# A two-layer hybrid backbone on one core: layer 2's adaLN moved to VectorE, the last down projection made token-major, and Fourier features taken two steps later

## The chip, the cores and the metric

The kernel runs on one core of a Trainium2 chip. The metric is the device time of one execution in microseconds (us), median of several executions. Engines are named as the profile names them: PE (TensorE, matmul), PEld (its weight loads), DVE (VectorE), ACT (ScalarE), POOL (GpSimd), SP (SyncE, which issues most DMAs).

## The reference, cut to what matters

Two layers over 256 context and 256 latent tokens of width 1024. Each layer normalizes, shifts and scales the tokens by six adaLN vectors of its own, mixes tokens in three branches (attention, Fourier, recurrence), and applies a ConvFFN:

```python
mx = jnp.split((silu_c @ w_ada[l] + b_ada[l])[:, None, :], N_MOD, axis=-1)   # latent: six vectors of 1024
mc = jnp.split(silu_cc @ w_ada[l] + b_ada[l], N_MOD, axis=-1)                # context
hx = modulate(rms_norm(x, norm_mix[l]), mx[0], mx[1])
x = x + mx[2] * merge(attention, fourier, recurrence, gates, w_out[l])
x = x + mx[5] * conv_ffn(modulate(rms_norm(x, norm_ffn[l]), mx[3], mx[4]), w_up[l], cw, cb, w_down[l])
# conv_ffn: u = depthwise_conv3(h @ w_up); up, gate = split(u); return (gelu(gate) * up) @ w_down
# in layer 1 the context tokens take the same steps with mc; layer 2 updates latent tokens only
return rms_norm(x, final_norm)
```

Layer 2 needs the context's vectors only for its first two chunks (shift and scale of the mixer's norm), and those of the latent tokens for all six. `w_ada[l]` is 1024 x 6144 (24 MB), `w_up` 1024 x 5632, `w_down` 2816 x 1024.

## The kernel before, in words

**Layout.** The residual stream `xr` is channel-major: eight tiles of 128 channels x 512 tokens. Every float32 product is made of three matmuls over high and low parts (`gemm`, L137): a weight tile is loaded by SP into one of three "raw" buffers (`chunk`, L161; `load`, L173, which also calls a tick), and `unit` (L192) splits it into a high part (cast, ACT) and a low part (subtraction, DVE), in a pool of three buffers each. So a tile of 128 output channels over 1024 inputs is 24 matmuls; with 512 tokens each has 512 columns, with 256 tokens (layer 2's second half) 256.

**Order of the work.** The order on each engine is fixed when the program is built, from priorities in program order; the DMAs of SP stay in program order. Layer 1's mixer runs to about 461 us of the profile, its output projection to 511; the first ConvFFN runs from 511 to 889 us (eight up/gate pairs of tiles, the first half of the down products with `down(0, 14)`, three more pairs, then `down(14, NF)`, L1142); layer 2's latent projections follow to 925, its attention to 1004, Fourier, merging and recurrence to 1172, output projection to 1199, and the second ConvFFN to the end (1404.5), in the same two halves.

**adaLN.** `ada_steps` (L354) makes one third of a layer's vectors: for each of eight row tiles of 128 rows it loads 128 x 2048 of `w_ada` (1 MB) and makes four float32 products with the two conditioning vectors `cvec` as a 32-column stationary block, side by side in one bank; a copy by DVE, four transposes and two bias adds end it. It is a generator: each `next` does one row tile. `spread(steps, rate)` (L398) makes every weight load advance the steps by `rate`. For layer 2, the first third runs in the first ConvFFN at rate 0.4 behind three empty steps, the parameters of layer 2 and `final_gains`, and what is left is emitted at its last down tile (L1167). The other two thirds (`steps_mix`, L1298) run in layer 2's mixer: one step per finished head in attention (`weighted`, L842) and at rate 0.5 in the merges.

**Attention and Fourier features.** `attention` (L771) walks over eight items (head pairs and heads) in steps k: scores of item k, transposes of item k - 1, weighted values of item k - 2. `FILLS[1]` says at which steps the Fourier features (`features`, L672, 2 x 3 steps: a load, then two groups of 24 matmuls) are put in.

**Down projection and end.** `finish` (L1095) makes the last down products of tile m (stationary: 128 x 128 of `w_down`; moving: 256 or 512 tokens of `gT`), then `residual` on DVE and the squares. In layer 2 `to_tokens` (L1212) scales each tile by the final gain and transposes it to token-major, and at the end the sum of squares is made on PE, and the rows are scaled and stored. `ffn` (L1119) uses five PSUM banks "mm" for projections and down products.

## Time and profile before

| | |
|---|---|
| median of 3 runs | 1407.57 us (1404.57 to 1408.45) |
| profiled execution | 1406.22 us, of which the span from the first to the last instruction is 1404.5 us |
| mean granted TensorE clock | 0.992 |
| PE / DVE / ACT / POOL busy | 1369.5 / 851.3 / 687.8 / 196.2 us |
| HBM | 193.5 MB read, 139 GB/s over the span |

All stretches below are in microseconds from the span's start. Matmuls are pipelined: the duration of a row is from the first column in to the last out, and the distance of two starts is what a matmul costs in a dense stream. "PEclk" is the granted clock as a share of 2.4 GHz.

### The profile page before, as it was taken

How to read it: one execution, taken by the hardware profiler on the slowest of the kernel's cores; microseconds unless marked ns; L12 is line 12 of the kernel's file. 1: busy time of each engine (PE TensorE's matmuls, PEld its weight loads, DVE VectorE, ACT ScalarE, POOL GpSimd, SP SyncE). 2: the span in 40 equal slices, each digit the busy share in tenths (PEclk: the TensorE clock that was granted, in tenths of full speed). 3: DMA queues.
4: the chain of work that ended last, by engine and by line, in shares of the span. 5: the costliest groups of instructions: out<-in, count | busy, mean ns of one | idle time of the engine just before them, and what ended most of it. 6: DMA issues, size and time to landing. Idle time of an engine off the chain costs nothing.

```text
span 1404.5 us, 20928 instructions
## 1 busy us (share of the span) xinstructions
PE 1369.5 (98%) x8362; PEld 1168.4 (83%) x8362; DVE 851.3 (61%) x1417; ACT 687.8 (49%) x1163; POOL 196.2 (14%) x195
## 2 busy tenths in 40 slices
PE   7999999999999999999999999999999999999997
PEld 6676598888888898888888877877788889999997
DVE  4587656656634565555543453778576676777575
ACT  5475635424523444444322442566477855566354
POOL 2011002003200111211100111010111222122012
PEclk9999999999999999999999999999999999999999
DMA  9423733223233502223243337225666766455643
GB/s 332 144 99 133 273 114 98 79 91 105 76 105 105 180 31 90 66 93 112 79 135 95 112 108 259 65 74 197 184 207 191 224 186 205 136 193 168 196 142 99
DMA packets 187937, 195.94 MB, mean 140 GB/s; under 512 B 9372, under 2 KB 178322, under 8 KB 182720
## 3 DMA queue, kind: packets, MB, share of 16 engines
q1 hardware_dynamic: 186624, 193.23, 43.3%
q0 software_dynamic: 1216, 1.38, 0.3%
q8 instruction: 65, 1.06, 0.3%
q14 instruction: 32, 0.26, 0.1%
HBM read 193.54 MB, written 1.05 MB: 139 GB/s over the span
## 4 chain that ended last, share of the span: by engine, by line
PE 90%; DVE 4%; DMA 3%; ACT 2%; issue 1%; SPq 0%; ACTq 0%; DVEq 0%
PE proj L129 54%; PE down L129 8%; PE out L129 7%; PE lat L129 4%; PE pa L129 4%; PE uf L129 2%; PE sc L129 2%; PE pv L129 2%; PE gt L129 1%; PE pt L834 1%; DMA raw<-in_w_ada_dram 1%; DMA raw<-in_w_down_dram 1%; PE kn L129 1%; PE v L129 1%; DMA raw<-in_w_in_dram 1%
## 5 line engine op out<-in xcount | busy, mean ns | idle before, releaser
L158 DVE TENSOR_TENSOR wl<-raw,wh 128x1024 fp32r<-128x1024 f32 (+9 forms) x339 | 335.5, 1003 | 190.5 <-ACT wh L151 186.3
L129 PE MATMUL proj<-hh,wh 128*128 128x512 f32 (+1 forms) x1232 | 416.3, 338 | 1.1 <-ACT hh L478 1.1
L129 PE MATMUL proj<-hh,wl 128*128 128x512 f32 (+1 forms) x1232 | 415.6, 338 | 1.8 <-DVE wl L158 1.8
L129 PE MATMUL proj<-hl,wh 128*128 128x512 f32 (+1 forms) x1232 | 415.9, 338 | 0.0
L151 ACT CAST wh<-raw 128x1024 fp32r<-128x1024 f32 (+7 forms) x307 | 249.6, 833 | 291.3 <-PE proj L129 168.8
L129 PEld LDWEIGHTS proj<-hh,wl 128*128 128x128 f32 x1232 | 234.8, 191 | 27.1 <-DVE wl L158 2.7
L129 PEld LDWEIGHTS proj<-hh,wh 128*128 128x128 f32 x1232 | 235.0, 191 | 26.5 <-ACT hh L478 1.3
L129 PEld LDWEIGHTS proj<-hl,wh 128*128 128x128 f32 x1232 | 234.9, 191 | 24.6
L1199 POOL TENSOR_TENSOR gate<-gate,up 128x512 f32<-128x512 f32 (+1 forms) x44 | 55.3, 1256 | 444.4 <-ACT gate L1198 423.7
L129 PE MATMUL down<-gTh,wh 128*128 128x512 f32 (+1 forms) x224 | 75.5, 337 | 0.0
L129 PE MATMUL down<-gTh,wl 128*128 128x512 f32 (+1 forms) x224 | 75.4, 337 | 0.0
L129 PE MATMUL down<-gTl,wh 128*128 128x512 f32 (+1 forms) x224 | 75.3, 336 | 0.0
L158 DVE TENSOR_TENSOR gTl<-gate,gTh 128x512 fp32r<-128x512 f32 (+1 forms) x44 | 24.6, 559 | 78.5 <-ACT gTh L151 78.5
L129 PE MATMUL pa<-raw,cvec 128*32 128x512 f32 (+1 forms) x576 | 63.9, 457 | 2.4 <-DMA raw<-in_w_ada_dram 2.4
L444 POOL TENSOR_TENSOR sq<-sq,sq 128x256 f32<-128x256 f32 (+1 forms) x28 | 31.6, 1128 | 201.1 <-ACT sq L442 201.1
L151 ACT CAST gTh<-gate 128x512 fp32r<-128x512 f32 (+1 forms) x44 | 22.6, 514 | 51.3 <-POOL gate L1199 51.3
L129 PE MATMUL out<-mh,wl 128*128 128x256 f32 (+1 forms) x152 | 47.4, 312 | 0.0
L129 PE MATMUL out<-mh,wh 128*128 128x256 f32 (+1 forms) x152 | 47.4, 313 | 0.0
L129 PE MATMUL out<-ml,wh 128*128 128x256 f32 (+1 forms) x152 | 47.4, 312 | 0.0
L129 PEld LDWEIGHTS down<-gTh,wh 128*128 128x128 f32 x224 | 42.5, 190 | 4.5
L129 PEld LDWEIGHTS down<-gTh,wl 128*128 128x128 f32 x224 | 42.5, 190 | 4.4
L129 PEld LDWEIGHTS down<-gTl,wh 128*128 128x128 f32 x224 | 42.5, 190 | 4.3
(288 smaller groups left out, 2631.6 us busy)
## 6 DMA issues: line engine op xcount, KB each, us to landing
raw<-in_w_up_dram SPq DMA_DIRECT2D x44, 1024.0 KB, 5.1
raw<-in_w_ada_dram SPq DMA_DIRECT2D x40, 1024.0 KB, 5.0
raw<-in_w_in_dram SPq DMA_DIRECT2D x30, 1024.0 KB, 5.6
raw<-in_w_down_dram SPq DMA_DIRECT2D x16, 896.0 KB, 5.1
raw<-in_w_ada_dram SPq DMA_DIRECT2D x32, 256.0 KB, 7.2
raw<-in_w_in_dram SPq DMA_DIRECT2D x16, 512.0 KB, 5.0
raw<-in_w_out_dram SPq DMA_DIRECT2D x8, 1024.0 KB, 5.2
raw<-in_w_down_dram SPq DMA_DIRECT2D x16, 512.0 KB, 3.9
```

The lines of the kernel that those rows point to most:

```text
L129: pinned(nc.tensor.matmul(o, lhsT, rhs, start=start, stop=stop))
L151: nc.scalar.copy(out, in_)
L158: (lo_eng or nc.vector).tensor_tensor(lo, src, hi, op=ALU.subtract)
L444: eng.tensor_tensor(self.terms[0][:, r], self.terms[0][:, r], sq[:, r], op=ALU.add)
L834: nc.tensor.transpose(o[:, c], probs[i][:, kt * P : (kt + 1) * P], ident)
L1199: nc.gpsimd.tensor_tensor(g, g, us[z], op=ALU.mult)
```

## The change

Five things. (1) Layer 2's adaLN is no longer made of matmuls with a 32-column block. `ada_vector` takes jobs of 512 columns by 1024 rows (both conditionings) or 1024 by 1024 (latent only); a chunk is 512 rows x 512 columns (1 MB). For each 128 rows, DVE multiplies the 128 x 512 weights by the conditioning value of that row (a scalar per partition) and adds them to an accumulator in SBUF; eight such operations make a sum per partition, and `summed` adds the partitions up with eight products of a 128 x 128 block with a column of ones, one job later, and adds the bias. There are four jobs of the first kind and four of the second: 24 chunks, 128 operations on DVE, 64 products on PE. (2) All of it runs in the first ConvFFN, at 2 steps per weight load in place of 0.4, behind the parameters and ten empty steps; layer 2's mixer has no such steps left. (3) In layer 2 the Fourier features' second half is put in at step 8 of attention, before at step 6. (4) Layer 2's down products are token-major: stationary is `gT` (128 tokens), moving are 512 columns of `w_down`, whose rows are loaded two row tiles at a time (1 MB); they accumulate in four banks over the whole loop, two tiles per pair from the second pair's turn on, the last four tiles after the loop; projections keep three banks. (5) The residual is transposed to token-major in the loop (`token_major`), gate and final gain are spread to rows, and the end is made in token-major: multiply, add, square with a sum per row, root, scale, store.

```diff
-FILLS = ({12: 1}, {2: 3, 6: 3})
+FILLS = ({12: 1}, {2: 3, 8: 3})
...
+            if tag != "rows" and i < 3:
+                yield
+                yield
...
+    def ada_vector(l, jobs):
+        cols = columns_of[l]
+        def fetch(job, i):
+            c0, half = job[0][i]
+            src = a["w_ada"][l][half * 512 : (half + 1) * 512, c0 : c0 + 512]
+            return chunk(src.rearrange("(k p) c -> p k c", p=P), 4, 512)
+        def summed(quarters, two):
+            o = bank("pa", "e")[:, 0:16].rearrange("p (g u r) -> p g u r", g=4, u=2)
+            for g, (z, c, *_) in enumerate(quarters):
+                for u in range(2):
+                    mm(o[:, g, u, :], two[z][:, c + u * P : c + (u + 1) * P], ones, True, True)
+            for g, (z, c, s, j) in enumerate(quarters):
+                blk, f = j // 16, j % 16
+                nc.vector.tensor_tensor(
+                    adas[l][blk][:, s, f : f + 2], o[:, g, :, 0], cols["b_ada"][:, j : j + 2], op=ALU.add
+                )
+        sums = None
+        for n, job in enumerate(jobs):
+            halves, quarters, todo = job
+            v = fetch(job, 0)
+            yield
+            accs = [slot("acc", t, F32) for t in ("aa", "ab")]
+            for i, (c0, half) in enumerate(halves):
+                after = fetch(job, i + 1) if i + 1 < len(halves) else None
+                for k in range(4):
+                    for z, s in todo[i]:
+                        w, sc = v[:, k, :], cvec[:, 4 * half + k, s : s + 1]
+                        if half == 0 and k == 0:
+                            nc.vector.tensor_scalar(accs[z], w, sc, None, op0=ALU.mult)
+                        else:
+                            nc.vector.scalar_tensor_tensor(accs[z], w, sc, accs[z], op0=ALU.mult, op1=ALU.add)
+                    if k == 1 and len(todo[i]) > 1:
+                        yield
+                if i == 0 and sums:
+                    summed(*sums)
+                v = after
+                yield
+            sums = quarters, accs
+        yield
+        summed(*sums)
...
+    def ada_both(chunk_of, part):
+        c0 = chunk_of * D + part * 512
+        quarters = [(s, o, s, (c0 + o) // P) for s in range(2) for o in (0, 256)]
+        return ((c0, 0), (c0, 1)), quarters, [[(0, 0), (1, 1)]] * 2
+    def ada_latent(chunk_of):
+        c0 = chunk_of * D
+        quarters = [(z, o, 1, (c0 + z * 512 + o) // P) for z in range(2) for o in (0, 256)]
+        return (
+            tuple((c0 + z * 512, half) for z in range(2) for half in range(2)),
+            quarters,
+            [[(z, 1)] for z in range(2) for _ in range(2)],
...
-            spread(steps, 0.4)
+            spread(steps, 2.0)
...
+        def row_of(cols):
+            t = slot("row", "row", F32, D)
+            for z in range(2):
+                o = bank("rowb", "mm")
+                for i in range(4):
+                    j = 4 * z + i
+                    mm(o[:, i * P : (i + 1) * P], cols[:, j : j + 1].to_broadcast([P, P]), ident, True, True)
+                nc.scalar.copy(t[:, z * 512 : (z + 1) * 512], o)
+            return t
...
+        def token_major():
+            rows_["gain"] = slot("row", "row", F32, D)
+            nc.gpsimd.dma_start(rows_["gain"], a["final_norm"].unsqueeze(0).to_broadcast([P, D]))
+            rows_["gate"] = row_of(ada_cols[2][:, 1, 8:16])
+            yield
+            rows_["x"] = [slot("xt", "row", F32, D) for _ in range(2)]
+            for tt in range(2):
+                for z in range(2):
+                    o = bank("xtb", "mm")
+                    for i in range(4):
+                        nc.tensor.transpose(
+                            o[:, i * P : (i + 1) * P], xr[4 * z + i][:, CTX + tt * P : CTX + (tt + 1) * P], ident
+                        )
+                    nc.scalar.copy(rows_["x"][tt][:, z * 512 : (z + 1) * 512], o)
+                yield
...
+        def down_weights(k, tag=None):
+            v = chunk(a["w_down"][l][k * P : (k + 2) * P, :].rearrange("(k p) c -> p k c", p=P), 2, D)
+            return [[x[:, 0] for x in unit(v[:, z : z + 1], tag)] for z in range(2)]
+        def down_part(k, w, tt, z):
+            if not accs:
+                accs.extend([bank("acc") for _ in range(2)] for _ in range(2))
+            q, c = slice(tt * P, (tt + 1) * P), slice(z * 512, (z + 1) * 512)
+            gemm(accs[tt][z], [(gT[k][0][:, q], gT[k][1][:, q], w[0][:, c], w[1][:, c])], k == 0, k == NF - 1)
+        def down_tokens(k):
+            ws = down_weights(k)
+            for i in range(2):
+                for tt in range(2):
+                    for z in range(2):
+                        down_part(k + i, ws[i], tt, z)
...
+        def down_last(k):
+            ws = {}
+            for k2 in range(k, NF, 2):
+                ws[k2], ws[k2 + 1] = down_weights(k2, "wd")
+            t = small.tile([P, 1], F32, tag="warm", name=nm("warm"), bufs=1)
+            nc.scalar.activation(t, gT[-1][1][:, 0:1].bitcast(F32), AF.Sqrt, bias=eps, scale=0.0)
+            first = NF - 2
+            for k2 in range(k, first):
+                for tt in range(2):
+                    for z in range(2):
+                        down_part(k2, ws[k2], tt, z)
+            ys, yg = [[[slot("y", "y", F32) for _ in range(2)] for _ in range(2)] for _ in range(2)]
+            ssq = small.tile([P, 2, 2], F32, tag="ssq", name="ssq", bufs=1)
+            for tt in range(2):
+                for z in range(2):
+                    for k2 in range(first, NF):
+                        down_part(k2, ws[k2], tt, z)
+                    with prio(150):
+                        c, y = slice(z * 512, (z + 1) * 512), ys[tt][z]
+                        nc.vector.tensor_tensor(y, accs[tt][z], rows_["gate"][:, c], op=ALU.mult)
+                        nc.vector.tensor_tensor(y, y, rows_["x"][tt][:, c], op=ALU.add)
+                        junk = slot("sq", "s", F32)
+                        nc.scalar.activation(junk, y, AF.Square, accum_out=ssq[:, tt, z : z + 1])
+                        e = nc.vector if tt and z else nc.gpsimd
+                        e.tensor_tensor(yg[tt][z], y, rows_["gain"][:, c], op=ALU.mult)
+                with prio(150):
+                    r = small.tile([P, 1], F32, tag="ry", name=nm("ry"), bufs=2)
+                    nc.vector.tensor_tensor(r, ssq[:, tt, 0:1], ssq[:, tt, 1:2], op=ALU.add)
+                    nc.scalar.activation(r, r, AF.Sqrt, bias=eps, scale=1.0 / D)
+                    nc.vector.reciprocal(r, r)
+                    nc.vector.tensor_scalar(yg[tt][0], yg[tt][0], r, None, op0=ALU.mult)
+                    nc.scalar.activation(yg[tt][1], yg[tt][1], AF.Copy, scale=r)
+                    for z in range(2):
+                        nc.sync.dma_start(out[0, tt * P : (tt + 1) * P, z * 512 : (z + 1) * 512], yg[tt][z])
...
+        if last:
+            side = token_major()
+            with phase("ffn", gT=16, c=8, row=4, wd=8, y=8):
+                with banks(acc=4, mm=3):
+                    next(side)
+                    for i in range(0, NF, 2):
+                        pair_of_tiles(i)
+                        if 2 <= i < NF - 2:
+                            down_tokens(i - 2)
+                        if i >= 4:
+                            next(side, None)
+                    down_last(NF - 4)
+            return
...
-    steps = chain(iter([None] * 3), params(1, nc.gpsimd), final_gains(), ada(1, 0))
+    for b in range(1, 3):
+        nc.gpsimd.memset(adas[1][b], 0.0)
+    par1 = params(1, nc.gpsimd)
+    parts_of = lambda chunks: [ada_both(c, part) for c in chunks for part in range(2)]
+    vec1 = ada_vector(1, parts_of((0, 1)) + [ada_latent(c) for c in range(2, 6)])
+    steps = chain(iter([None] * 2), islice(par1, 2), iter([None] * 8), par1, vec1)
...
-    steps_mix = chain(ada(1, 1), ada(1, 2))
```

## Rows read from the trace of the kernel before

**Rows 1.** The page, busy time of the engines (us, share, instructions), and its chain by engine
```profile
PE 1369.5 (98%) x8362; PEld 1168.4 (83%) x8362; DVE 851.3 (61%) x1417; ACT 687.8 (49%) x1163; POOL 196.2 (14%) x195
...
PE 90%; DVE 4%; DMA 3%; ACT 2%; issue 1%; SPq 0%; ACTq 0%; DVEq 0%
```

**Rows 2.** Stretch, length, busy us (count) of PE, PEld, DVE, ACT, POOL; PEclk, DMA share, GB/s
```profile
511.30:686.20 174.90, 174.90 (x816) 146.49 (x816) 98.74 (x125) 75.92 (x101) 26.08 (x28) 1.00 0.28 88
686.20:763.10 76.90, 76.90 (x341) 63.30 (x340) 30.79 (x66) 19.38 (x23) 1.36 (x2) 1.00 0.37 110
...
925.00:1004.20 79.20, 77.63 (x498) 58.49 (x498) 58.51 (x135) 45.33 (x114) 7.09 (x9) 0.98 0.39 130
1004.20:1107.00 102.80, 102.65 (x722) 91.97 (x722) 72.26 (x93) 77.21 (x105) 16.57 (x16) 1.00 0.68 209
1107.00:1131.00 24.00, 22.22 (x165) 18.79 (x164) 15.32 (x21) 18.54 (x26) 8.22 (x9) 1.00 0.57 178
...
1369.40:1404.50 35.10, 27.06 (x217) 25.71 (x215) 19.37 (x39) 15.65 (x32) 8.01 (x8) 0.94 0.32 98
```

**Rows 3.** The same by stretch, of the instructions on adaLN's tile pa alone, summed
```profile
sum 619.70, PE 30.53 PEld 4.51 DVE 1.38 ACT 0.00; mean PE 3.82 PEld 0.56 DVE 0.17 ACT 0.00
...
925.00:1004.20 79.20, 13.72 (x64) 1.91 (x64) 0.69 (x1) 0.00 (x0) 0.98 0.39 130
```

**Rows 4.** Timeline of PE around one row tile: start, duration, instruction
```profile
806.63 0.39 PE L129 MATMUL proj<-hh,wl 128*128 128x512 f32 x1
806.95 1.06 PE L129 MATMUL pa<-raw,cvec 128*32 128x512 f32 x8
...
808.28 0.39 PE L129 MATMUL proj<-hl,wh 128*128 128x512 f32 x1
```

**Rows 5.** Groups by shape: transposes on PE (count, then busy us and mean ns)
```profile
L834 PE MATMUL pt<-ident,pr 128*128 128x128 f32 x160 | 26.5, 278 | 0.0
```

**Rows 6.** PE's waits, 760 to 890 us: in all, times, longest
```profile
PE pa L129 <- DMA raw<-in_w_ada_dram: 1.8, 1, 1.8
```

**Rows 7.** Timeline of PE around four products of a 128x128 block with ones
```profile
912.74 0.28 PE L129 MATMUL lat<-hh,wl 128*128 128x256 f32 x1
913.16 1.02 PE L129 MATMUL ss<-ones,sq 128*128 128x2 f32 x8
...
914.25 0.28 PE L129 MATMUL lat<-hl,wh 128*128 128x256 f32 x1
```

**Rows 8.** Groups on DVE by shape, and one tile's durations (min/median/max)
```profile
L822 DVE TENSOR_SCALAR pr<-pr,rs 128x512 f32<-128x512 f32 x24 | 11.7, 487 | 0.3
...
L479 DVE SCALAR_TENSOR_TENSOR hl<-hf,ada,hh 128x256 fp32r<-128x256 f32 x56 | 26.2, 492 | 0.2 <-ACT hh L478 0.2
...
L512 DVE SCALAR_TENSOR_TENSOR nf<-lr,cols,rb 128x512 f32<-128x512 f32 x7 | 4.9, 745 | 3.2 <-PE rb L129 3.2
...
L953 DVE SCALAR_TENSOR_TENSOR ri<-ri,u x16: 684/692/1125, 222.4 to 1116.9; 128x512 f32<-128x512 f32 x16
```

**Rows 9.** Pieces of the chain: dense streams of 512 and of 256 columns
```profile
708.39 54.71 PE down L129 x241
...
1294.57 40.32 PE down L129 x336
```

**Rows 10.** Timeline of DVE and of POOL, 226 to 229 us
```profile
227.52 1.15 DVE L952 SCALAR_TENSOR_TENSOR ri<-a,ri 128x512 f32<-128x512 f32 x1 [2.92 <-ACT ri L949]
...
226.08 2.04 POOL L951 TENSOR_TENSOR a<-av 128x512 f32<-128x512 f32 x2 [12.11 <-ACT av L947]
```

**Rows 11.** DMA issues: count, size of each, us to landing
```profile
raw<-in_w_ada_dram SPq DMA_DIRECT2D x40, 1024.0 KB, 5.0
```

**Rows 12.** The end: the last down matmul, and the stores
```profile
1396.07 0.28 PE L129 MATMUL out<-gTh,wl 128*128 128x256 f32 x1
...
out_dram<-y SPq DMA_DIRECT2D x4, 256.0 KB, 2.5
```

More of the change, by code (lines that the diff above doesn't have):

```diff
@@ L1 @@
 import math
+from itertools import islice
 from contextlib import ExitStack, contextmanager
@@ L96, in phase @@
             was = {t: where.get(t) for t in tags}
-            where.update({t: (pool, n) for t, n in tags.items()})
+            where.update({t: (pool, n, t) for t, n in tags.items()})
             yield
@@ L297, in spread_out @@
             pp = bank("pp", "lat" if tag == "rows" and i == 0 else "e")
[L298 removed]
+            ins = nc.tensor.transpose(pp[:, 0:n], rows4[0:n, i, :], ident[0:n, 0:n])
+            if tag == "rows":
+                tc.keep_in_program_order(ins)
             cols = par.tile([P, n], F32, tag=f"cols{i}", name=nm("cols"))
@@ L1027, in project_out @@
             first()
-            finish(held, merged, ranges(t0), gate, t0, squares, None, then)
+            finish(held, merged, ranges(t0), gate, t0, squares, then)
         def out_units():
@@ L1093, in ranges, with finish @@
         return [slice(r.start - t0, r.stop - t0) for r in streams(t0)]
-    def finish(held, xs, qs, gate, t0, squares, also=None, then=None, cut=0):
+    def finish(held, xs, qs, gate, t0, squares, then=None, cut=0):
         os = [bank("out")[:, 0 : T - t0] for _ in held]
@@ L1143, in down @@
             held, gate = [], ada_cols[2][:, :, 8:16]
-            together = 3 if last else 2
+            together = 2
             for m in range(8):
@@ L1160, in down @@
                     if together - 1 <= m < HELD[l]:
-                        finish(
-                            held, gT[k0:k1], [Y], gate, t0, squares, to_tokens if last else None,
-                            cut=k1 - k0 - 2 if len(held) > 1 else 0,
-                        )
+                        finish(held, gT[k0:k1], [Y], gate, t0, squares, cut=k1 - k0 - 2 if len(held) > 1 else 0)
                     if m == 7:
@@ L1168, in down @@
                             first()
-                        finish(held, gT[k0:k1], ranges(t0), gate, t0, squares, to_tokens if last else None, then)
+                        finish(held, gT[k0:k1], ranges(t0), gate, t0, squares, then)
                 else:
@@ L1180, in first_pair @@
         def first_pair():
-            two = [(next(ups), bank("proj", "mm")[:, 0:W]) for _ in range(2)]
+            two = [(next(ups), bank("proj", "acc" if last else "mm")[:, 0:W]) for _ in range(2)]
             for q in streams(t0):
@@ L1188, in first_pair, with pair_of_tiles @@
             return [conv(o, z, "up") for z, (u, o) in enumerate(two)]
-        with phase("ffn", gT=32, c=8), banks(dict(out="mm"), mm=5, rb=2):
-            for i in range(0, NF, 2):
-                if i == 0:
-                    us = first_pair()
-                else:
-                    us = [conv(project(next(ups), h, X), i + z, "up") for z in range(2)]
-                for z in range(2):
-                    g = conv(project(next(gts), h, X), NF + i + z, "gate")
-                    nc.scalar.activation(g, g, AF.Gelu_apprx_tanh)
-                    nc.gpsimd.tensor_tensor(g, g, us[z], op=ALU.mult)
-                    hi, lo = pair("gT", "gT", W)
-                    split(hi, lo, g)
-                    gT.append((hi, lo))
+        def pair_of_tiles(i):
+            if i == 0:
+                us = first_pair()
+            else:
+                us = [conv(project(next(ups), h, X), i + z, "up") for z in range(2)]
+            for z in range(2):
+                g = conv(project(next(gts), h, X), NF + i + z, "gate")
+                nc.scalar.activation(g, g, AF.Gelu_apprx_tanh)
+                nc.gpsimd.tensor_tensor(g, g, us[z], op=ALU.mult)
+                hi, lo = pair("gT", "gT", W)
+                split(hi, lo, g)
+                gT.append((hi, lo))
+        if last:
[11 more added lines that the diff above has]
+            return
+        with phase("ffn", gT=32, c=8, aa=2, ab=2), banks(dict(out="mm"), mm=5, rb=2):
+            for i in range(0, NF, 2):
+                pair_of_tiles(i)
                 if i == 14:
@@ L1206, in ffn @@
         ticks.clear()
-    fn = const.tile([P, 8], F32, tag="fn", name="fn")
-    ys = []
-    def to_tokens(j):
-        if not ys:
-            ys.extend([slot("y", "h", F32) for _ in range(2)] for _ in range(2))
-        f = slot("yf", "n", F32)
-        nc.vector.tensor_scalar(f[:, 0:SEQ], xr[j][:, CTX:], fn[:, j : j + 1], None, op0=ALU.mult)
-        pt = bank("yt", "rb")
-        for i in range(2):
-            nc.tensor.transpose(pt[:, i * P : (i + 1) * P], f[:, i * P : (i + 1) * P], ident)
-        for i in range(2):
-            c = slice((j % 4) * P, (j % 4 + 1) * P)
-            copy((nc.vector, nc.scalar)[i], ys[i][j // 4][:, c], pt[:, i * P : (i + 1) * P])
     columns_of = [{} for _ in range(DEPTH)]
@@ L1306, in backbone @@
     emit(mix)
[L1307 to L1316 removed]
+    ffn(1, columns_of[1], adas[1], True, h_ffn1, ups1, None, None, None, None)
 _INS = [
```

28 lines of the change are left out of this document (5 added, 23 removed).

## The prediction

> **What bounds the kernel now.** Read the page first: PE is busy 98% of the span, DVE 61%, and the chain that ended last is PE for 90% of its length [rows 1]. So time is PE's instruction stream, and the sum below is made of what enters and leaves that stream, and of holes in it. Next read the table by stage [rows 2]. In the first ConvFFN (511 to 763 us) PE is busy all the time; in layer 2's attention (925 to 1004) and where the branches end (1107 to 1131) there are holes of about 2 us; the last stretch of the kernel (1369 to 1404.5) has 8 us without a matmul, nearly all of it the tail. DVE, which is to get the new work, is busy 98.7 of 174.9 us in the first stretch of the first ConvFFN and 58.5 of 79.2 us in layer 2's attention. The granted clock is 1.00, the upper level of 2.4 GHz, in the first ConvFFN, and 0.98 or more up to 1131.
>
> **Layer 2's adaLN leaves PE.** It was 24 row tiles of four products each; the trace has them as 8 matmuls a tile. PE's busy time with them is 30.5 us over five stretches (187 of the 192 matmuls) [rows 3]; with the last five, 31.5. A look at one tile agrees: the matmul before it starts at 806.63, the next but one after it at 808.28, 1.65 us where 0.45 would do, so 1.2 us a tile [rows 4]. Term: **-31.5**. Twelve transposes of the row sums and one of the final gain go too; a transpose of that shape is 26.5 us by 160 or 0.17 us [rows 5]: **-2**. Between 760 and 890 us PE waits once, 1.8 us, for the chunk of a row tile [rows 6]; the change has fetched all before, so **-2**.
>
> **What comes instead on PE.** Eight jobs each end in eight products of a 128x128 float32 block with a column of ones. The nearest row is the sum of squares: four such products are 8 matmuls in 1.02 us, and set in a stream of 0.12 us matmuls they move it by 1.27 us (912.74 to 914.25, where 0.24 would do) [rows 7]. For 64 products that is 16.3 us at the bare rate and 20.3 at the whole price of each group of four; a job has two groups back to back, so I take 17.5: **+17.5**.
>
> **What comes on DVE.** 128 operations on 128x512 (per job 2 of the two-operand form, 14 with an accumulator). The first form took 487 ns. For the second no row has both its size and a pointer scalar: from SBUF without a pointer it is 692 ns (median), with a pointer at 128x256 it is 492 ns, at 128x512 with one operand in PSUM 745 ns [rows 8]. I take 0.745: 112 x 0.745 + 16 x 0.487 = 91 us, with the small bias adds some 96. Whether PE sees it depends on where it falls. The rate of 2 steps per weight load spends 19 steps on parameters and pauses; the 42 steps of the sum then cover the last 2.75 up/gate pairs before the first down half, that half, and the 3 pairs after it. A pair of tiles is 4 x 24 matmuls at 0.227 us [rows 9], or 21.8 us of PE, plus 1.7 for the new products of 0.8 jobs: 23.5. DVE's own work in a pair is 98.7 / 8 = 12.3 [rows 2]; four steps add 12.8 operations and some adds, 9.6. Sum 21.9, against 23.5. In the down half a load has 9.6 us of PE (76.9 / 8) and 3.9 of DVE, plus 4.9: no conflict.
>
> The 1.6 us left in a pair are not safe. GpSimd multiplies gate and up in a pair twice, today in a gap of DVE. Where GpSimd and DVE ran together, a DVE operation of the form that otherwise takes some 690 ns took 1.15 us, and GpSimd's two took 2.04 [rows 10]. Two such meetings cost a pair some 1 to 2 us and close the gap. The Trainium skill ("GPSIMD Engine Reference", Specifications) says the same: GpSimd shares its SBUF interfaces with VectorE, and they contend when an instruction of DVE has two SBUF inputs; the trace agrees. And DVE executes in order, so an accumulate that waits for its chunk holds the convolutions and the low halves of the weights behind it, and through those PE. The chunks share the three "raw" buffers and SP's queue with the weights, 1 MB each, 5.0 us to landing [rows 11]. Bound from below 0 (DVE fits), from above 20 us, some 3.5 us for each of 5.75 pairs. I take 1 us a pair: **+6**.
>
> **What the removed products had covered.** In layer 2's attention the row tiles stood in places where PE would otherwise have waited for a softmax: 13.7 us of busy time there for 64 matmuls, 1.7 us a tile against 1.2 in a dense stream [rows 3, 4]. Without them PE has some 64 us of work there and DVE 58.5, in step with each other through the score and transpose banks. Items 6 and 7, which have neither projections nor, now, Fourier features, are the likeliest holes; the features, moved to step 8, fill the drain behind the last scores. I give back 4 us of the 13.7 (bounds 0 and 10). From 1004 to 1133 the tiles stood among projections; only at 1107 to 1131, with 1.8 us idle [rows 2], is a recurrence late anyway: 2 back (bounds 0 and 4). Term: **+6**. What runs on SP's queue there loses 16 transfers of 1 MB; nothing waits longer for that.
>
> **The last ConvFFN.** Its down products turn from 528 matmuls of 256 columns at 0.120 us (40.3 / 336), 63.4 us, into 264 of 512 columns at 0.227, 59.9 [rows 9]: -3.5. The 16 transposes of the result and the last sums of squares leave (about -3); 16 transposes of the residual, in the loop, and 8 broadcasts of the gate come (+3, of which the broadcasts may lie in the wait for the norm at 1198). Small waits for weights of the last stretch shrink, since half of the down weights are now loaded among the pairs: -1. The tail stays: today 8.2 us from the last down matmul at 1396.1 to the end, over residual, square, sum, root, scaling and a 2.5 us store [rows 12]; afterwards multiply, add, square, root, scaling and the same store, 7.5 to 8.5. The projections have three PSUM banks in place of five: a bank is held for the 2.9 us of its 24 matmuls and until the convolution on ACT and DVE has read it, behind their other work; no row shows that with three banks, so 0 to 4, taken as +0.5 since five banks left no hole in the loop before. Together **-4**.
>
> **The sum.** -31.5 - 2 - 2 + 17.5 + 6 + 6 - 4 = -10. Against the profiled execution (1406.2 us, 0.1% under the median) that is 1396.2; against the median of 1407.57, **1397.5**.
>
> **Rivals.** *One: DVE becomes the bound of the first ConvFFN.* An accumulate that stands at the head of DVE's queue before its chunk has landed holds DVE for up to the 5 us of a landing. About 14 chunks fall into the 5.75 pairs, which leave DVE 1.6 us each, or 9 us. It decides from 0.7 us a chunk on; at 2.5 us a chunk PE loses 35 - 9 = 26 us instead of 6, and the kernel takes 1417, slower. For it: three raw buffers for two consumers, and a DVE load of 93% before contention. Against: weights are split up to three units ahead, and the chunks are fetched one ahead.
> The Trainium skill has a rule that would end there as well ("Vector Engine (DVE) Microarchitecture Reference", Points that are easy to get wrong): the accumulate form with two SBUF sources that are not bf16 runs at half throughput. The mechanism in rows: 256 more columns cost 745 - 492 = 253 ns; at half throughput 512 columns would cost 506 more, 1.25 us each, a pair 27.5 us of DVE against 23.5 of PE, and the time 1415, or 1423 with the down loads, which then exceed PE too. But the 692 ns of [rows 8] are of this form with two float32 sources in SBUF, so the rows speak against it: 3 in 100, inside this rival's chance.
> *Two: the removed products were only filling.* If attention and branches return 10 + 9 of their 24.5 us rather than 6, the time is 1410, no different. For it: the spread places of the tiles in attention; against: the branches' PE is full (102.65 of 102.80 us) [rows 2].
> *Three: all cover holds.* No stall in the first ConvFFN, 2 given back in place of 6: 1387.5. For it: the averages, and two to three units of lookahead.
>
> **How the numbers follow.** Forecast 0.52, one 0.16, two 0.13, three 0.19. The forecast's own spread is 1392 to 1404. The range reaches to three below and to two above, and stops short of most of one: **1386 to 1411**. A measurement here tells about 0.3% (4 us) from no change. Faster by more than that: nearly all of the forecast and of three, **0.69**; within: two's lower half and the forecast's upper end, **0.14**; slower: one and the rest of two, **0.17**.
>
> **What would show it.** Right: no matmul of a 32-column block on w_ada after 800 us, 128 of two columns in the first ConvFFN for 16 to 20 us; layer 2's attention some 9 us shorter and its branches some 9; the first ConvFFN 8 to 12 us longer in all, DVE over 85% busy in its later pairs; the second ConvFFN about 4 us shorter, with 512-column down matmuls 0.227 us apart. Wrong: PE waiting for the low halves of weights or for convolutions in the first ConvFFN by tens of us, a granted clock under 1.00 there, accumulates near 1.2 us, or attention as long as before.

## The result, and the profile after

The changed kernel takes 1387.0 us (median of 4 runs, 1384.1 to 1387.7) against 1408.0 for the kernel before: a ratio of 0.985 (95% interval 0.982 to 0.987), 21 us faster. The forecast was 10 us (1397.5, in a range from 1386 to 1411). The direction was right and the time lies just inside the range, but the gain that was forecast is half of the one that came.

The page of the changed kernel, its busy times and its chain, answers to [rows 1]:

```profile
PE 1345.7 (97%) x8029; PEld 1161.8 (84%) x8029; DVE 935.8 (68%) x1545; ACT 687.5 (50%) x1160; POOL 200.2 (14%) x194
...
PE 90%; DVE 4%; ACT 2%; DMA 2%; issue 1%; SPq 0%; POOL 0%; ACTq 0%; DVEq 0%
```

PE lost 24 us of busy time, DVE gained 84, and the chain is PE's as before. Where the time went is seen by stage. The first fence is the kernel before, the second the changed one, in the same stages: first ConvFFN, latents with attention of layer 2, its branches, output projection, second ConvFFN to the end (columns as in [rows 2]).

```profile
509.90:889.40 379.50, 376.04 (x1807) 309.29 (x1807) 190.88 (x286) 144.06 (x197) 45.18 (x45) 1.00 0.36 113
...
889.40:1003.40 114.00, 110.67 (x725) 88.20 (x724) 81.33 (x182) 64.19 (x159) 9.72 (x13) 0.98 0.34 112
1003.40:1171.60 168.20, 165.95 (x1221) 150.65 (x1222) 115.81 (x158) 115.65 (x162) 29.89 (x28) 1.00 0.68 209
1171.60:1199.30 27.70, 25.28 (x205) 24.57 (x204) 16.61 (x25) 13.90 (x23) 8.43 (x6) 0.99 0.59 191
1199.30:1404.50 205.20, 197.12 (x1608) 195.63 (x1608) 142.59 (x225) 114.33 (x183) 32.43 (x28) 0.97 0.50 154
```

```profile
511.60:894.40 382.80, 380.79 (x1866) 322.15 (x1866) 282.39 (x447) 144.75 (x198) 44.85 (x40) 1.00 0.50 159
...
894.40:999.00 104.60, 97.60 (x656) 85.83 (x655) 79.07 (x176) 62.16 (x157) 9.78 (x13) 0.97 0.19 53
999.00:1156.20 157.20, 155.32 (x1153) 148.47 (x1154) 114.22 (x152) 115.19 (x162) 33.43 (x28) 1.00 0.55 164
1156.20:1184.80 28.60, 27.67 (x221) 27.02 (x221) 17.55 (x27) 14.78 (x24) 8.96 (x7) 0.97 0.63 203
1184.80:1384.60 199.80, 190.10 (x1338) 178.79 (x1337) 138.05 (x201) 114.65 (x178) 29.79 (x25) 0.98 0.48 159
```

| stage | before | after | difference | the forecast's terms there |
|---|---|---|---|---|
| to the first ConvFFN (same work) | 509.9 | 511.6 | +1.7 | 0 |
| first ConvFFN | 379.5 | 382.8 | +3.3 | +12.5 |
| latents, attention of layer 2 | 114.0 | 104.6 | -9.4 | -10.4 |
| branches of layer 2 | 168.2 | 157.2 | -11.0 | -8.2 |
| output projection, second ConvFFN | 232.9 | 228.4 | -4.5 | -4 |
| sum | 1404.5 | 1384.6 | -19.9 | -10 |

(The forecast's column puts each term where its work lies: row tiles -8.3 / -13.7 / -9.5 by [rows 3], transposes about -0.7 a stage, the wait -2, products +17.5 and VectorE +6 in the first ConvFFN, the holes +4 and +2.) The first row is layer 1, which no edit touches; over the profiles of this study it lay between 509.9 and 513.1, so 1 to 3 us of any profile's difference are that. The first ConvFFN of the same code is 384.4 us in two other profiles (e3, e9). Nine of the ten missing microseconds are in the first ConvFFN.

**There the price of the products and the stalls were both too high.** This is PE around one job's eight products (start, duration, instruction), which answers to [rows 7]:

```profile
666.47 0.39 PE L130 MATMUL proj<-hh,wl 128*128 128x512 f32 x1
666.70 1.84 PE L130 MATMUL pa<-ones,acc 128*128 128x2 f32 x16
668.40 0.49 PE L130 MATMUL proj<-hh,wh 128*128 128x512 f32 x1
668.72 0.40 PE L130 MATMUL proj<-hl,wh 128*128 128x512 f32 x1
```

From 666.47 to 668.72 pass 2.25 us where two matmuls would take 0.45: 1.8 us a job, the same for all eight jobs of the trace, or 14.4, not 17.5. The sum of the stage is then already there: -8.3 - 0.7 - 2 + 14.4 = +3.4, against +3.3 measured. Nothing is left for stalls, within the 1.6 us by which this stage differs between profiles. PE has no wait of its own between 590 and 845 us in this trace.

**VectorE is nearly as full as forecast, and PE does not notice.** Four of the stretches of 22 to 24 us that have sums:

```profile
612.00:634.00 22.00, 22.00 (x99) 18.18 (x98) 19.15 (x25) 8.94 (x12) 3.27 (x2) 1.00 0.62 200
634.00:656.00 22.00, 22.00 (x98) 18.23 (x98) 21.17 (x52) 10.91 (x15) 2.92 (x2) 1.00 0.53 182
656.00:678.00 22.00, 22.00 (x106) 18.49 (x106) 19.10 (x30) 9.83 (x14) 2.67 (x2) 1.00 0.44 144
...
797.00:821.00 24.00, 24.00 (x118) 20.21 (x117) 22.72 (x33) 9.38 (x13) 2.55 (x2) 1.00 0.62 210
```

DVE is busy 87 to 96% of them (third busy number; the forecast had 93% of a pair before contention), PE all the time, with the clock at its upper level. The accumulates, by their tile (least, median and longest duration in ns, first and last start):

```profile
L440 DVE SCALAR_TENSOR_TENSOR acc<-raw,cvec,acc x112: 731/746/1783, 606.4 to 825.1; 128x512 f32<-128x512 f32 x112
```

What DVE waited for between 590 and 845 us, of its waits (total, times, longest):

```profile
DVE acc L438 <- DMA raw<-in_w_ada_dram: 2.8, 5, 0.8
...
DVE acc L440 <- DMA raw<-in_w_ada_dram: 1.0, 2, 0.6
```

The median of 746 ns is the 745 taken from [rows 8]. The chunks held DVE for 3.8 us in all, not 2.5 us each as the first rival had it.

### The profile page after: what moved, and what is told of

The parts are those of the page before. It is cut to its first block, busy times and chain, and to the rows that moved or that the text cites. A ratio compares the mean times of both kernels' runs of the same rounds, so it can differ in the third digit from the quotient of the medians.

```text
span 1384.6 us, 20366 instructions
## 1 busy us (share of the span) xinstructions
PE 1345.7 (97%) x8029; PEld 1161.8 (84%) x8029; DVE 935.8 (68%) x1545; ACT 687.5 (50%) x1160; POOL 200.2 (14%) x194
## 4 chain that ended last, share of the span: by engine, by line
PE 90%; DVE 4%; ACT 2%; DMA 2%; issue 1%; SPq 0%; POOL 0%; ACTq 0%; DVEq 0%
PE proj L130 54%; PE out L130 7%; PE down L130 6%; PE acc L130 4%; PE lat L130 4%; PE pa L130 3%; PE uf L130 2%; PE pv L130 2%; PE sc L130 2%; PE gt L130 1%; PE pt L904 1%; DMA raw<-in_w_ada_dram 1%; PE kn L130 1%; PE v L130 1%; DVE hf L547 1%
## 5 line engine op out<-in xcount | busy, mean ns | idle before, releaser
L440 DVE SCALAR_TENSOR_TENSOR acc<-raw,cvec,acc 128x512 f32<-128x512 f32 x112 | 88.6, 809 | 2.5 <-DMA raw<-in_w_ada_dram 1.0
L514 POOL TENSOR_TENSOR sq<-sq,sq 128x256 f32<-128x256 f32 (+1 forms) x22 | 25.8, 1170 | 178.9 <-ACT sq L512 178.9
L1347 ACT ACTIVATE gate<-gate 128x512 f32<-128x512 f32 (+1 forms) x44 | 23.1, 525 | 54.9 <-DVE gate L1205 54.3
L154 DVE CAST wh<-raw 128x1024 fp32r<-128x1024 f32 x32 | 22.4, 700 | 33.1 <-PE proj L130 32.5
L130 PE MATMUL down<-gTh,wh 128*128 128x512 f32 x112 | 44.1, 394 | 0.0
L130 PE MATMUL down<-gTh,wl 128*128 128x512 f32 x112 | 43.7, 390 | 0.0
L130 PE MATMUL down<-gTl,wh 128*128 128x512 f32 x112 | 43.6, 390 | 0.0
L130 PE MATMUL lat<-hh,wh 128*128 128x512 f32 (+3 forms) x108 | 38.4, 355 | 0.1
```

Source lines behind the costliest of these rows:

```text
L130: pinned(nc.tensor.matmul(o, lhsT, rhs, start=start, stop=stop))
L154: eng.tensor_copy(out, in_)
L440: nc.vector.scalar_tensor_tensor(accs[z], w, sc, accs[z], op0=ALU.mult, op1=ALU.add)
L514: eng.tensor_tensor(self.terms[0][:, r], self.terms[0][:, r], sq[:, r], op=ALU.add)
L1347: nc.scalar.activation(g, g, AF.Gelu_apprx_tanh)
```

## The experiments

Theory S, in e1's words: VectorE's sums are hidden whole, the products cost their bare rate, and the removed row tiles yield all their time. Its figures say less than that: 35.5 us less 14.1 for 128 matmuls at 0.11 would be 21 us, and its 14 to 17 us leave 4 to 7 for holes that it does not name. Theory F is the forecast's account: stalls of 1 us a pair, 17.5 us for the products. Times are medians; "changed" is 1387.0 us, and each run's ratio is against the kernel before, run beside it. The changed kernel was not run beside them; the median of the kernel before moved from 1407.5 to 1408.8 between such groups of runs.

**e1_ada_only.** The kernel before with the first two parts of the change alone (`ada_vector` in the first ConvFFN at rate 2.0):

```diff
-    steps = chain(iter([None] * 3), params(1, nc.gpsimd), final_gains(), ada(1, 0))
-    steps_mix = chain(ada(1, 1), ada(1, 2))
+    steps = chain(iter([None] * 2), islice(par1, 2), iter([None] * 8), par1, final_gains(), vec1)
+    steps_mix = iter(())
```

> The kernel before with layer 2's adaLN on VectorE in the first ConvFFN alone; the last down projection stays channel-major, the Fourier features stay at step 6. Theory S (VectorE's sums are hidden whole, the products on PE cost their bare rate of 0.11 us a matmul, the removed row tiles yield all their time): 14 to 17 us faster than before, 1391 to 1394, first ConvFFN 2 to 5 us longer than before. Theory F (as forecast: 6 us of stalls from VectorE, 17.5 for the products, 6 given back): 6 us faster, 1402, first ConvFFN about 13 us longer.

Measured 1393.6 us against 1407.7: ratio 0.991 (0.989 to 0.993), 14 us faster. Its first ConvFFN is 4.7 us longer than before:

```profile
510.00:894.20 384.20, 382.31 (x1868) 323.01 (x1867) 280.68 (x448) 145.04 (x198) 46.05 (x42) 1.00 0.50 158
```

Both figures are S's, at the lower end of its gain, and neither is F's: the stalls are absent. Attention gave back more than S's words allow (latents and attention 105.7 us, 8.3 less than before).

**e2_down_only** and **e11_down_same_steps.** The kernel before with the token-major down projection alone. The first also lost the two steps of the old final gain, so that the row tiles of adaLN came two steps earlier; the second keeps them in place:

```diff
-    steps = chain(iter([None] * 3), params(1, nc.gpsimd), final_gains(), ada(1, 0))
+    steps = chain(iter([None] * 3), params(1, nc.gpsimd), ada(1, 0))                      # e2
+    steps = chain(iter([None] * 3), params(1, nc.gpsimd), iter([None] * 2), ada(1, 0))    # e11
```

> The kernel before with the token-major last down projection alone; adaLN stays on PE as before, the Fourier features at step 6. Theory S (the last ConvFFN's part adds to the others unchanged): 5 to 6 us faster than before, 1402 to 1403, all of it in the second ConvFFN. Forecast: 4 us faster. Rival: the two parts need each other (PE with the clock at its upper level from an earlier start, fewer transfers before): under 2 us faster.

> The kernel before with the token-major last down projection alone, as in e2_down_only, but with two empty steps where the steps of the final gain stood, so that the row tiles of layer 2's adaLN stand at the same loads of the first ConvFFN as before. If the down projection is worth its 5 us alone and e2_down_only lost them to row tiles that moved (2.9 us in the first ConvFFN), this is 4 to 5 us faster than before: 1402.5 to 1403.5. If the part is worth nothing without the other one: within 2 us of before.

e2 took 1406.1 us, no different from before (0.9994, 0.998 to 1.001); e11 took 1402.0 against 1408.8 (0.995, 0.994 to 0.997), 6.8 us faster. The trace of e2, second and first ConvFFN:

```profile
1205.20:1404.90 199.70, 189.65 (x1339) 178.08 (x1337) 138.00 (x200) 114.72 (x179) 30.05 (x25) 0.99 0.48 159
513.10:895.50 382.40, 378.63 (x1805) 311.66 (x1805) 192.34 (x288) 145.03 (x198) 45.82 (x45) 0.99 0.36 113
```

Its second ConvFFN has about the 199.8 us of the changed kernel; but the first grew from 379.5 to 382.4 us without new work on PE. In e11's profile it is 378.6. Near the end of this stage e2's profile has a wait of PE for squares that GpSimd adds (1.9 us in one wait), and the granted clock is then at its lower level of 1.2 GHz for 7 us:

```profile
PE ss L130 <- POOL sq L511: 1.9, 1, 1.9
...
880.50:887.40 6.90, 6.90 (x35) 6.90 (x35) 1.69 (x5) 1.24 (x4) 0.00 (x0) 0.51 0.17 64
```

e11's profile does not have this wait. So the down projection is worth 5 us alone by e11's profile (second ConvFFN 200.1 us against 205.2) and 7 by its median, and moving the row tiles by two steps ate some 4 of them (3.8 in the first ConvFFN of the two profiles, 4.1 between the medians). That the move makes GpSimd's squares late is read from one profile of each and was not tested further; the part of e2's loss that lies before 510 us is scatter.

**e3_fills6.** The changed kernel with one number back:

```diff
-FILLS = ({12: 1}, {2: 3, 8: 3})
+FILLS = ({12: 1}, {2: 3, 6: 3})
```

> The changed kernel with the second half of the Fourier features back at step 6 of layer 2's attention. If the features at step 8 fill the drain behind the last scores, as forecast, taking them back costs 2 to 4 us, all in layer 2's attention: 1389 to 1391. Rival (PE's work in attention is in step with VectorE either way, the place doesn't matter): 1387 within 1 us.

Measured 1389.1 us, 2.1 more than the changed kernel; the four runs of each just touch (1387.5 to 1391.7 against 1384.1 to 1387.7). In its profile latents and attention take 107.8 us in place of 104.6:

```profile
895.60:1003.40 107.80, 99.51 (x656) 86.92 (x656) 79.52 (x176) 62.12 (x157) 9.79 (x13) 0.96 0.18 51
```

PE is idle 8.3 us of it in place of 7.0, and 1.9 us longer busy: the clock is at its lower level for 3.4 us more, from 996.7 us on. Attention and branches together are 264.9 us here, 264.3 in e1 (step 6 as well) and 261.8 in the changed kernel. So step 8 is worth 2 to 3 us.

**e7_no_rowtiles.** The kernel before, with the products of row tiles 1 to 7 of each third left out:

```diff
-                mm(pa[32 * j : 32 * j + 32, :], cvec[:, k, :], v[:, 0, 512 * j : 512 * (j + 1)], k == 0, k == 7)
+                if l == 0 or k == 0:
+                    mm(pa[32 * j : 32 * j + 32, :], cvec[:, k, :], v[:, 0, 512 * j : 512 * (j + 1)], k == 0, l == 1 or k == 7)
```

> The kernel before with 21 of the 24 row tiles of layer 2's adaLN left out on PE (only the first of each third is multiplied; all chunks are still loaded, nothing is put in their place). It prices the removal alone. Whole yield (21 of 24 of 31.5 us, and the wait for a chunk): 27 to 30 us faster, 1378 to 1381. Forecast (6 of it given back as holes): 22 to 24 us faster, 1384 to 1386. Rival two (the tiles were filling): 10 to 15 us faster, 1393 to 1398.

Measured 1387.7 us, 20 us faster than before: 2 us short of the forecast's window, between it and rival two. By stage: first ConvFFN 370.9 us (-8.6), attention and branches

```profile
881.80:990.30 108.50, 99.39 (x669) 85.71 (x668) 79.41 (x181) 62.42 (x157) 9.90 (x13) 0.98 0.38 128
990.30:1151.80 161.50, 159.62 (x1165) 151.99 (x1166) 115.22 (x155) 115.17 (x162) 31.76 (x28) 0.98 0.68 211
```

-5.5 and -6.7. In attention one tile of eight stayed, so about 12 us of PE's 13.7 went, and the stage is 5.5 us shorter: 6 to 7 us were filling. With the features still at step 6, that is more than the forecast's 4; e3 shows that the features at step 8 return 2 to 3 of them. Both together are near the forecast's 4, and the changed kernel's profile shows it directly: PE is idle 7.0 us of its latents and attention, 3.3 before.

**e4_twice, e5_half_more, e12_quarter_more.** How far is VectorE from binding? All 112 accumulates, 64 of them or 32 of them are done a second time into a tile nobody reads:

```diff
+                            # e4: always; e5: if k % 2; e12: if k == 3
+                            nc.vector.scalar_tensor_tensor(scrap, w, sc, accs[z], op0=ALU.mult, op1=ALU.add)
```

> The changed kernel with each of the 112 accumulates on VectorE done twice (the second into a tile that nobody reads): 84 us more on VectorE, nothing else. If VectorE binds as soon as its work in a stretch exceeds PE's (pairs 30.3 us against 23.3, down loads 13.0 against 10.3), PE loses 40 to 61 us: 1427 to 1448. If VectorE's room is that of the whole first ConvFFN (all its idle time usable), under 20 us more: below 1407.

> The changed kernel with every second accumulate on VectorE done twice: some 42 us more there. Forecast's account (each pair that VectorE overfills costs PE the difference, 26.1 against 23.3 us in 5.75 pairs, 10.9 against 10.3 in the down loads): 12 to 21 us slower than the changed kernel, 1399 to 1408. Theory S (weights are split two to three units ahead and the accumulates fill VectorE's idle time, so a stretch of some 90% costs nothing and a small excess is absorbed): 0 to 6 us slower, 1387 to 1393.

> The changed kernel with every fourth accumulate on VectorE done twice: some 21 to 24 us more there. By the account of pairs (24.0 us of VectorE against 23.3 of PE in 5.75 pairs, 9.9 against 10.3 in the down loads) 3 to 5 us slower than the changed kernel, 1390 to 1392. If there is room left in the changed kernel, 0 to 2 us slower. If any overfilled pair makes a hole that also takes PE's clock to its lower level, 7 us or more.

By the pages VectorE's busy time grows by 21 us in e12 (956.8 against 935.8), by 45 in e5 (981.1; the 42 that were expected stand for 56 second sums, and k % 2 takes 64) and by 76.5 in e4 (1012.3). With 21 us more the kernel takes 1385.3 us, no slower than the changed one; with 45 more 1403.9, 17 us slower; with 76.5 more 1441.2, 54 us slower. First e12 by stretch, 590 to 845 us, then e5 by stretch (columns as before):

```profile
590.00:692.00 102.00, 102.00 (x469) 84.87 (x467) 92.99 (x152) 41.17 (x54) 11.65 (x8) 1.00 0.46 149
692.00:774.00 82.00, 82.00 (x387) 68.67 (x386) 74.25 (x122) 17.53 (x21) 4.26 (x2) 1.00 0.71 222
774.00:845.00 71.00, 71.00 (x339) 59.57 (x338) 62.42 (x93) 27.73 (x35) 8.68 (x5) 1.00 0.65 211
```

```profile
692.00:789.00 97.00, 92.14 (x420) 76.57 (x419) 89.87 (x144) 18.46 (x22) 3.15 (x2) 0.95 0.64 197
...
700.00:720.00 20.00, 15.51 (x57) 12.83 (x56) 19.86 (x34) 3.04 (x4) 1.86 (x1) 0.74 0.49 152
```

And what PE waited for in e5 between 590 and 890 us (total, times, longest):

```profile
PE pa L130 <- DVE acc L441: 4.4, 1, 4.4
PE proj L130 <- ACT wh L152: 2.4, 2, 1.4
```

At 88 to 91% of each long stretch VectorE costs PE nothing. In e5 it is 99% busy from 700 to 720, and there PE waits once, 4.4 us, for an accumulator: the products stand in PE's queue in a fixed place, and the extra sums make them late. The granted clock falls at the end of this wait (0.74 in that stretch; the lower level, 1.2 GHz, from 708 to 718), so the hole is paid twice. Theory S (0 to 6 us, and under 20 for e4) is excluded here. The account by pairs gave times that came for e5 (12 to 21 us) and e4 (40 to 61), and was 3 to 5 us too dear for e12. But it knows no clock: of the 20 us by which e5's first ConvFFN is longer than the changed kernel's, some 8 are waits of PE and most of the rest is the lower clock. That its sums fit is partly luck.

**e6_one_product and e8_single_pass.** What the products cost:

```diff
-            for g, (z, c, *_) in enumerate(quarters):
-                for u in range(2):
-                    mm(o[:, g, u, :], two[z][:, c + u * P : c + (u + 1) * P], ones, True, True)
+            mm(o.rearrange("p g u r -> p (g u r)"), two[0][:, 0:P], ones16, True, True)
```

That is e6: one product with 16 columns of ones for a job's eight; it leaves out the sums of the other seven blocks. In e8 the ones and each job's finished sums are float32r (the accumulators have one buffer each in place of two, the finished sums two):

```diff
+    ones_r = const.tile([P, 2], F32R, tag="ones_r", name="ones_r")
+    nc.vector.tensor_copy(ones_r, ones)
-                    mm(o[:, g, u, :], two[z][:, c + u * P : c + (u + 1) * P], ones, True, True)
+                    mm(o[:, g, u, :], two[z][:, c + u * P : c + (u + 1) * P], ones_r, True, True)
-                            nc.vector.scalar_tensor_tensor(accs[z], w, sc, accs[z], op0=ALU.mult, op1=ALU.add)
+                            last_one = half == 1 and k == 3
+                            if last_one:
+                                sums_r[z] = slot("accr", ("ra", "rb_")[z])
+                            nc.vector.scalar_tensor_tensor(
+                                sums_r[z] if last_one else accs[z], w, sc, accs[z], op0=ALU.mult, op1=ALU.add
+                            )
-            sums = quarters, accs
+            sums = quarters, sums_r
```

> The changed kernel with one product in place of the eight that add a job's sums over the partitions (the result of the others is left out): 56 of 64 products less, VectorE unchanged. At the bare rate of the trace (16 matmuls in 1.8 us) it is 12.6 us faster than the changed kernel, 1374 to 1375; at the forecast's price 15 us, 1371 to 1372. If PE were held by VectorE there, removing PE's work would gain little: under 5 us.

> The changed kernel with the products over the partitions in the reduced form: the last accumulate of a job writes the type that PE takes in one matmul in place of two, so 64 matmuls less at 0.11 us. 6 to 8 us faster than the changed kernel if PE's stream sets the time of the first ConvFFN: 1379 to 1381. Under 2 us if VectorE or the weight loads bind there.

e6 took 1379.8 us, 7.2 less than the changed kernel and 5.4 short of the 12.6 that the bare rate gives. Its trace has 1.9 us of PE waiting for a weight's high part and 1.2 for low parts in the down half, which the changed kernel has not, and the granted clock is at its lower level for 3.4 us there (713.4 to 716.8), which costs some 1.7 us more: together 4.8 of the 5.4. e8 removes half of the matmuls (64 remain in its trace, of the same 250 ns), took 1378.3 us, 8.7 less than the changed kernel and 29 less than the kernel before (0.980, 0.978 to 0.981), and PE has no such wait. Its first ConvFFN is 375.8 us, 7.0 less than the changed kernel's, which is the price of 64 matmuls at 0.11 us; the other 1.7 us of the medians lie outside that stage, within the scatter.

**e9_fill9 and e10_both.** The last third of the second features at step 9, in the changed kernel and in e8:

```diff
-FILLS = ({12: 1}, {2: 3, 8: 3})
+FILLS = ({12: 1}, {2: 3, 8: 2, 9: 1})
```

> The changed kernel with the last third of the second half of the Fourier features at step 9 of layer 2's attention in place of step 8. The holes that are left behind the last scores (two of 1.0 to 1.1 us before the last weighted values) lie after step 8: if they are waits for the last softmax, this fills them and is 1 to 2 us faster than the changed kernel. Rival: the features' own low halves are then late for the Fourier products that follow, no gain or up to 1 us slower.

> The single-pass products and the features at step 9 together. Single-pass alone was 8.7 us faster than the changed kernel; together 9 to 11 us faster, 1376 to 1378.

1387.5 us and 1377.4 us: no gain over their counterparts that can be told. In e9's profile latents and attention are 1.2 us shorter (103.4): a wait of PE of 0.9 us before the last weighted values, at 996.6 in the changed kernel, is gone. The branches are 1.4 us longer, and not by the rival's late low halves, for PE's waits there have not grown (idle 1.8 us against 1.9). It is the clock: behind the hole at the end of the recurrence it is at its lower level for 3.4 us, where the changed kernel's profile (second row) has the upper one:

```profile
1116.20:1119.60 3.40, 3.40 (x18) 3.40 (x17) 3.13 (x4) 0.18 (x1) 1.22 (x1) 0.51 0.67 181
...
1116.20:1119.60 3.40, 3.40 (x29) 3.40 (x30) 3.34 (x4) 1.08 (x3) 1.01 (x1) 1.00 0.62 168
```

e10's profile has it too (1106.5 to 1109.9), and so has e1's with the features at step 6 (1117.8 to 1121.2); whether step 9 brings it is open. e8 or e10 is the version to keep, 29 to 31 us faster than the kernel before.

## Why the prediction was wrong in size, point by point

**The removal was right.** Row tiles, transposes and the wait for a chunk were priced at 35.5 us of PE, from PE's busy time with them [rows 3, 4, 5, 6]. The stages return -11 (first ConvFFN, before the new products), -9.4 and -11.0; that is the forecast's price less 4 us of holes.

**"What the removed products had covered": half right.** Attention gave back 4 us, as forecast, and e7 with e3 shows how: 6 to 7 without the move of the features, 2 to 3 less with it. The 2 us for the branches were wrong: they became 11.0 us shorter where 10.2 were priced for tiles and transposes, and PE's idle time there did not grow (1.9 us against 2.3), so no hole opened at all. In e7 it did not grow either (1.9); its branches are only 6.7 us shorter, with the clock lower there (0.98 against 1.00). The stretch with 1.8 us idle in [rows 2] still has its hole of 1.7 us, while the recurrence ends; it was there with the tiles as well and is not a price of removing them.

**"What comes instead on PE": the term was mis-sized.** 17.5 against 14.4 measured. What the forecast called the bare rate, 1.02 us for 8 matmuls, runs from the first one's start to the last one's end; one such matmul lasts 0.25:

```profile
L129 PE MATMUL ss<-ones,sq x76: 170/251/272, 61.0 to 1398.1; 128*128 128x2 f32 x76
```

Their starts are thus (1.02 - 0.25) / 7 = 0.11 us apart, and 16 of them cost 1.76 us, which is the price that came. The rest of the 1.27 us in [rows 7] is mostly a gap ahead of the group: it starts 0.42 us after the matmul before it (913.16 against 912.74), where 0.12 is the distance in the stream. In the changed kernel that distance is 0.23 (666.47 to 666.70), the stream's own, so no such gap is paid.

**"What comes on DVE" is the step that failed.** Its account of VectorE was good: 0.745 us an operation (746 measured), 93% of a pair before contention. Its next sentences charged the contention with GpSimd to PE, as 1 us a pair or +6, and none of this came. The contention that it read from [rows 10] is there: at 800.9 three accumulates beside a GpSimd multiply take 3.22 us, where three at 808.1 take 2.32, and the multiply takes 1.79, where the median of its line is 1.29:

```profile
801.80 1.79 POOL L1348 TENSOR_TENSOR gate<-gate,up 128x512 f32<-128x512 f32 x1 [5.37 <-ACT gate L1347]
...
800.92 3.22 DVE L440 SCALAR_TENSOR_TENSOR acc<-raw,cvec,acc 128x512 f32<-128x512 f32 x3
...
808.07 2.32 DVE L440 SCALAR_TENSOR_TENSOR acc<-raw,cvec,acc 128x512 f32<-128x512 f32 x3
...
L440 DVE SCALAR_TENSOR_TENSOR acc<-raw,cvec,acc 128x512 f32<-128x512 f32 x112 | 88.6, 809 | 2.5 <-DMA raw<-in_w_ada_dram 1.0
```

Seven of the 112 accumulates took 1.66 to 1.78 us, each of which started while GpSimd multiplied; the others took 0.73 to 0.76. The mean is 809 ns against the median of 746, so the contention is 112 x 0.063 = 7 us. The forecast's 6 was right as a cost of VectorE. But these 7 us fell on VectorE, which had 1.6 us a pair to spare, and PE, whose weights are split ahead into three buffers, saw none. A charge on an engine with slack had been entered as a charge on the bound. How much slack there is can be read from ScalarE, which makes the weights' high parts. When it waits until PE has freed a buffer, the weights are ahead (waits between 590 and 845 us; the changed kernel, then e12):

```profile
ACT wh L152 <- PE down L130: 35.9, 10, 5.7
ACT wh L152 <- PE proj L130: 33.0, 10, 4.5
...
ACT wh L152 <- PE proj L130: 14.8, 7, 4.5
ACT wh L152 <- PE down L130: 9.6, 2, 8.5
```

That is 69 us in the changed kernel and 24 in e12: 21 us more on VectorE use up part of this lead and leave PE untouched. e5 shows that VectorE does bind with 45 more. The Trainium skill's rule on the shared SBUF interfaces ("GPSIMD Engine Reference", Specifications) is borne out by these rows; its rule on half throughput for two SBUF sources that are not bf16 ("Vector Engine (DVE) Microarchitecture Reference", Points that are easy to get wrong) is not: this form has two float32 sources in SBUF here and takes 746 ns at the median for 512 columns, where the forecast worked out 1.25 us for half throughput.

**The rivals.** One did not happen: the chunks were a rival for DVE's queue for 3.8 us in all. VectorE can be made to bind, as e5 shows, but by more sums and not by chunks: from somewhere between 21 and 45 us of further sums on, with an accumulator as what PE waits for longest. Two is excluded by e1 and by the branches. Three (1387.5, all cover holds) is the time that came, but that its number fits is partly luck: the stalls were absent as it says, the holes (4 us, where it has 2) were not, and the products, which it prices at 17.5 us like the forecast, were 3 us cheaper.

**The last ConvFFN.** -4 forecast, -4.5 measured with the output projection. That is 0.9 us longer in this profile with the broadcast of the gate behind it, but only 0.2 in e3's and e6's, which have the same code there. The parts of the stage differ from the forecast's. The tail grew: from the start of the last down matmul to the end are 9.9 us, where it was 8.4; from its end, as the forecast's 8.2 was taken, 9.6, where 7.5 to 8.5 was forecast. The last down matmul on PE and the tail on DVE:

```profile
1374.65 0.39 PE L130 MATMUL acc<-wh,gTl 128*128 128x512 f32 x1
...
1376.30 0.67 DVE L1314 TENSOR_TENSOR y<-acc,row 128x512 f32<-128x512 f32 x1
1376.88 1.05 DVE L1325 TENSOR_SCALAR y<-y,ry 128x512 f32<-128x512 f32 x1
1377.85 0.68 DVE L1315 TENSOR_TENSOR y<-y,xt 128x512 f32<-128x512 f32 x1
1378.57 0.69 DVE L1319 TENSOR_TENSOR y<-y,row 128x512 f32<-128x512 f32 x1
```

The last block's product with the gate starts 1.3 us after its matmuls are through (1376.30 against 1374.65 + 0.39), and its addition waits behind the scaling of the first row tile. The matmuls made up for that: PE is busy 190.1 us of the second ConvFFN in place of 197.1, 7.0 less, where the terms of the forecast come to 3.5. Some 2 us of this are the clock, which is at its lower level for the first 6.2 us of the stage before and for 1.8 us after; the rest is not traced. PE's idle time grew by 1.6 us (9.7 against 8.1), and it is the tail in both. Three PSUM banks in place of five cost nothing that the trace shows: PE has no wait between 1184 and 1375 us. Reordering the tail was not tried.

## What to carry to other kernels

A cost on an engine that is not the bound is a charge against its own slack first: subtract it from that slack by stretch, and enter only what is left over on the bound. When work is moved from the bound to an idle engine, price what the removed work was covering (here 6 to 7 of 24 us, of which a filler at the right step returned 2 to 3), and the mending of the new form on the bound (here 14 us, half of which a single-pass form saves). Before two changes are called independent or not, hold the schedule between them fixed: two empty steps were worth some 3 to 5 us here (e2 against e11).

## What the runs showed that was not expected

VectorE could be loaded to 91% over 100 us of a PE-bound stage without PE losing anything (e12), and at 99% in one stretch of 20 us PE lost twice: the wait itself and the clock. In e5 PE's waits in the first ConvFFN add up to about 8 us more than in the changed kernel, and the stage is 20 us longer; the granted clock is at its lower level in it from 708 to 718, 834 to 841 and 851 to 855 us, 20 us in which matmuls of 512 columns start 0.43 us apart in place of 0.227. And VectorE's contention with GpSimd is not spread evenly: 105 of the 112 accumulates paid nothing, and seven took more than twice their time.
